# Moving the expert selection, the up bias and one weight split in a fixed engine order, and gathering the first expert in two steps

## The chip, the cores and the metric

One core of a Trainium2 chip runs the whole kernel. TensorE multiplies (its weight loads are listed apart), VectorE (DVE) and ScalarE (ACT) work elementwise, GpSimd (POOL) issues the scatter, and SyncE (SP) issues nearly all weight transfers on one in-order queue. The metric is device microseconds of one execution, the median of the runs. Before the change it is 1568.97 us (1568.40, 1568.97 and 1569.36).

## The reference

The computation is a decoder block for 512 tokens of width 1024: two mixing branches, a merge and a projection, then a mixture of experts with 32 experts of which each token takes four. Only the second half matters here:

```
h2 = rms_norm(x) * (1 + sc2) + sh2
logits = h2 @ w_router + b_router                  # 512 x 32
top 4 logits per token, softmax over them = gates
for each expert e, on the tokens that chose it:
    hu = h2 @ w_up[e] + b_up[e]                    # 1024 -> 2048, even columns x_glu, odd x_lin
    act = clamp(x_glu) * sigmoid(1.702 * x_glu) * (clamp(x_lin) + 1)
    y = act @ w_down[e] + b_down[e]                # 1024 -> 1024
    x[token] += g2 * gate * y
```

Weights and inputs are float32, and each expert has 8 MB of up weights and 4 MB of down weights.

## The kernel before

**Number format.** A float32 product is made of three float16 products: each operand is split into a high and a low half. A weight slab of 1 MB arrives in a staging slot (`st`). `split` (lines 330 to 345) lets ACT write the high half into another slot (line 341), then VectorE the low half (line 342); then the staging slot is free. Each expert has eight up slabs and four down slabs. The last down slab is multiplied in float32 without a split, so there are eleven splits per expert.

**Slots.** There are 18 slots of 8 KB per partition: the names `slot`, `slotb` and `slotc`. At most twelve hold staged weights; the others hold the split halves. A transfer is issued as soon as its slot is free (`pump`), in the order of use, so SP's queue waits for whatever frees that slot.

**Routing.** 512 tokens are four tiles of 128. For each tile `logits` projects, transposes and multiplies with the router, `choose` takes the four largest, builds a one-hot matrix and counts each token's place `pos` within its expert, `make_h2` writes the normalised tokens in two halves (the low half on GpSimd, line 997), and `gates` makes the softmax.

**Gather.** `select(e)` builds a one-hot matrix `sel` (tokens x 96 places) on VectorE (line 1125). `pick` multiplies h2 with it, 64 matmuls in four banks (line 1106), which ACT copies to `xg` (line 1113). Four small matmuls and three VectorE operations give the token index and gate.

**Expert loop.** For expert e, eight steps `up_k` accumulate in four banks `pu` that ACT has filled with the bias (`up_bias`, line 1138). At steps k = 2, 4, 5, 6 and 7 one piece of the next expert's gather is put in: the selection first, then its four banks. `swiglu` (lines 1153 to 1167) turns `pu` into `act`. Then `down_j` runs for the expert before (lines 1184 and 1192), with one `up_bias` after each of its four slabs, and `finish` writes y (line 1204), which GpSimd adds to the output by an indirect transfer (line 1196). At each step `ahead` splits the next slab, about six steps before its use.

**Order.** Up to `open_banks` a planner orders the instructions. From the mark behind `open_banks` on, every instruction of TensorE, VectorE and ACT is chained to the one written before it for the same engine. What is written first runs first.

Of the kernel before, what the change touches and what calls it, by code (L numbers as in the profile page):

```python
# [10 lines left out]
F32 = mybir.dt.float32  # L11
F16 = mybir.dt.float16
BF = mybir.dt.bfloat16
I32 = mybir.dt.int32
# [9 lines left out]
NT = 4  # L24
# [17 lines left out]
def block_body(tc, x, c, positions, w_ada, b_ada, norm1_gain, w_in, lower_bound_logits, hg_norm_gain,  # L42
# [19 lines left out]
    with top:  # L62
# [21 lines left out]
        def free(t):  # L84
            free_slots.append(t)
            staged[0] -= 1
            pump()
# [244 lines left out]

        def split(key, n, view_in=None, view_hi=None, keep=False):

            st = ready.pop(key)
            slot, hl = hl_take()
            src = st[:, :n] if view_in is None else view_in(st)
            hi, lo = hl[:, :n], hl[:, 2048:2048 + n]
            if view_hi is not None:
                hi, lo = view_hi(hi), view_hi(lo)  # L340
            A.activation(hi, src, AF.Copy, scale=SW)  # L341
            V.scalar_tensor_tensor(lo, src, SW, hi, op0=OP.mult, op1=OP.subtract)  # L342
            free(st)
            hlmap[key] = hl
            hlslot[key] = slot

        def hl_done(key):
# [570 lines left out]
        iota_c = moe.tile([128, 128], F32, name="iota_c")  # L918
        G.iota(iota_c, pattern=[[1, 128]], base=0, channel_multiplier=0, allow_small_or_imprecise_dtypes=True)
        tokn = wk.tile([128, NT], F32, name="tokn")  # L920
# [57 lines left out]

        def choose(t):
# [7 lines left out]
            pb = sd_bank()  # L987
# [3 lines left out]
            V.tensor_scalar(pos[:, t, :], pos[:, t, :], -1.0, None, op0=OP.add)  # L991
# [45 lines left out]

        def split_up(e, k):
            split(("up", e, k), 2048, view_in=lambda t: t.rearrange("p (f g) -> p g f", g=2),
                  view_hi=lambda t: t.rearrange("p (g f) -> p g f", g=2))  # L1040
# [8 lines left out]

        def ahead(i):  # L1050
            while cut[0] < len(order) and cut[0] <= i + LOOK and free_slots:
                o = order[cut[0]]
                if o[0] == "up":
                    split_up(o[1], o[2])
                elif o[2] < 3:
                    split(o, 2048)
                cut[0] += 1
# [6 lines left out]
        bias_dn()  # L1064
        pre(0)
        for t in range(NT):
            logits(t, ((0, D),) if t < NT - 1 else LAST)
# [7 lines left out]
        choose(NT - 1)  # L1075
        make_h2(NT - 1)
        if "lg" in dbg:
            G.dma_start(dbg["lg"], lg)
            G.dma_start(dbg["h2"], h2)

        if "pos" in dbg:
            G.dma_start(dbg["pos"], pos)
            G.dma_start(dbg["aux"], aux)
        w2p.close()
        psA.close()
        moe = top.enter_context(tc.tile_pool(name="moeb", bufs=1, reuse_waits="tile"))


        more_slots(moe, "slotc", NSC, NS + NSB + NSC - NHX)
        pse = top.enter_context(tc.tile_pool(name="pse", bufs=1, space=PSUM, reuse_waits="tile"))  # L1090
        pu = [pse.tile([128, 512], F32, name=f"pu{i}") for i in range(4)]
        pd = [pse.tile([128, 512], F32, name=f"pd{i}") for i in range(2)]

        def pick(sel, auxv):
# [5 lines left out]
            for part in range(2):  # L1100
                for u in range(2):
# [12 lines left out]
                    if not (part and u):  # L1114
                        yield None
            a = bk[:C, 4 * C:4 * C + 3]
# [4 lines left out]
            yield xg, gate[:, 2:3], idx  # L1121

# [6 lines left out]
        def open_banks():  # L1129

            z = moe.tile([128, 512], F16, name="sg_g", bufs=2)
            V.memset(z, 0.0)
            for i in range(4):
                T.matmul(pu[i], lhsT=z[:, :128], rhs=z, start=True, stop=True)

# [11 lines left out]

        def swiglu(act, act32):
            n = 4 * C
            g, l, s = [], [], []  # L1150
            for hf in range(2):
                g.append(moe.tile([128, n], F32, name="sg_g", bufs=2))
                V.tensor_scalar(g[hf], pu[hf][:, :n], 1.702 / SU, 7.0 * 1.702, op0=OP.mult, op1=OP.min)
                s.append(moe.tile([128, n], F32, name="sg_s", bufs=2))
                A.activation(s[hf], g[hf], AF.Silu)
            for hf in range(2):
                l.append(act32.rearrange("p k c -> p (k c)") if hf else moe.tile([128, n], F32, name="sg_l"))
                V.tensor_scalar(l[hf], pu[2 + hf][:, :n], -7.0 * SU, 7.0 * SU, op0=OP.max, op1=OP.min)
            parts = []
            for hf in range(2):  # L1160
# [48 lines left out]
        def overflow_table():  # L1209
# [9 lines left out]
            while C * q < S:  # L1219
# [10 lines left out]
            V.tensor_tensor(cmpt, iota_c[:, :NB, None].to_broadcast([128, NB, NE]),  # L1230
                            cum[:, None, :].to_broadcast([128, NB, NE]), op=OP.is_ge)
            eix = moe.tile([128, NB], F32, name="eix")
# [11 lines left out]
            V.tensor_sub(beg, iota_c[:, :NB], beg)  # L1244
            V.tensor_scalar(beg, beg, 1.0, float(C), op0=OP.add, op1=OP.mult)
            hl_give(slot)
# [16 lines left out]
        traced = nc.cur_bb.bb.instructions  # L1263
        marks = {}
        mark = traced[-1]
        first = prepare(0)
        next(first)
        gates(NT - 1)
        for _ in first:
            pass  # L1270
        for b in range(4):
            up_bias(bu[:, 0], b)
        i = 0
        for e in range(NEX + 1):
            if e < NEX:
                xg, gate, idx = state[e]
                prep = prepare(e + 1) if e + 1 < NEX else iter(())
# [7 lines left out]
            if e < NEX:  # L1285
# [4 lines left out]
            if e == 0:  # L1290
                for b in range(4):
                    up_bias(bu[:, 1], b)
            if e == NEX:
                tables = overflow_table()
            if e > 0:
                _, gate, idx = state.pop(e - 1)
                down_bias(E64[:, e - 1:e])
                for j in range(4):
                    ahead(i)
                    key = ("dn", e - 1, j)  # L1300
                    if j >= 3:
                        down_j(ready[key], j, *acts[e - 1])
                        free(ready.pop(key))
                    else:
# [6 lines left out]
                acts.pop(e - 1)  # L1311


        begin = next(n for n in reversed(range(len(traced))) if traced[n] is mark) + 1
# [11 lines left out]
        with tc.For_i(0, nreg, 1) as it:  # L1326
# [4 lines left out]
            ohb = moe.tile([128, NE], F32, name="ovo")  # L1331
            V.tensor_scalar(ohb, iota_c[:, :NE], col[:, 0:1], None, op0=OP.is_equal)
            pm = moe.tile([128, NT, NE], F32, name="ovm")
# [86 lines left out]
```

## Time and profile before

| what | value |
|---|---|
| median of the runs | 1568.97 us |
| profiled execution, its own time | 1569.14 us |
| its span, first to last instruction | 1567.3 us |
| mean granted TensorE clock | 0.984 of full speed |
| busy: TensorE, weight loads, VectorE, ACT, GpSimd | 90%, 66%, 84%, 67%, 21% |
| bytes read from HBM | 463.22 MB |
| start of the first expert's first up matmul | 452.44 us |

The routing of the last tile ends at about 446 us, the expert loop takes the time from there to 1553 us, and the rest is the last scatter. In the steady part of the loop one expert follows the other every 34 us. A row of a timeline gives the start, the duration, the engine, the line, the operation, output<-inputs, shapes and a count; in brackets stands how long the engine was idle before it and what it waited for.

### The profile page before, as it was taken

To read this page: it belongs to the slowest core of one execution; us is meant where nothing else is said; L and a number is where in the kernel's file an instruction comes from. 1 tells how busy PE (TensorE), PEld (TensorE's weight loads), DVE (VectorE), ACT (ScalarE), POOL (GpSimd) and SP (SyncE) were. 2 spreads that over 40 slices of the span, in tenths; PEclk is the share of its full clock that TensorE was granted. 3 is DMA by queue.
4 is the path that set the end of the run, shared out by engine and by line. 5 is a ranking of instruction groups with operands and counts; after the bars stand their busy time and mean duration, and the time that the engine had idled before them with its cause. 6 is when DMAs were issued, how large, how long until landed. Compare 5 with 4: busy or idle time off the path is not lost. (4 is left out here: it accounts for less than half of the span.)

```text
span 1567.3 us, 41129 instructions
## 1 busy us (share of the span) xinstructions
PE 1406.7 (90%) x18200; PEld 1036.1 (66%) x18200; DVE 1310.0 (84%) x1458; ACT 1052.6 (67%) x1022; POOL 331.5 (21%) x83
## 2 busy tenths in 40 slices
PE   4989999999948999999999999999989999999996
PEld 2546566445448777777777777777777777777783
DVE  6875675877977889998898999898989889898985
ACT  4555326423457778787778787877878787887871
POOL 1010000011110022233222233322223322222310
PEclk9999999999978999999999999999999999999998
DMA  9813312669368999999999999999999999999970
GB/s 319 274 54 97 105 42 72 214 216 321 148 245 307 342 387 367 383 383 378 380 382 373 378 384 382 377 377 376 377 382 378 381 378 389 378 373 372 384 287 15
DMA packets 113520, 476.44 MB, mean 304 GB/s; under 512 B 10717, under 2 KB 35386, under 8 KB 80538
## 3 DMA queue, kind: packets, MB, share of 16 engines
q1 hardware_dynamic: 106160, 458.78, 75.7%
q0 software_dynamic: 5440, 12.72, 3.8%
q8 instruction: 144, 2.36, 0.6%
q10 hardware_dynamic: 1738, 2.27, 0.4%
q14 instruction: 38, 0.31, 0.1%
HBM read 463.22 MB, written 14.70 MB: 305 GB/s over the span
## 5 line engine op out<-in xcount | busy, mean ns | idle before, releaser
L1196 POOL DMA_INDIRECT out_dram<-y,idx x32 | 296.0, 9249 | 814.0 <-DVE y L1204 779.3
L1145 PE MATMUL pu<-xg,slot 128*128 128x96 f16 x6192 | 283.2, 207 | 25.5 <-ACT pu L1138 25.1
L342 DVE SCALAR_TENSOR_TENSOR slot<-slot,slot 128x2048 f16<-128x2048 f32 (+1 forms) x111 | 252.0, 2272 | 55.3 <-ACT slot L341 51.4
L1145 PEld LDWEIGHTS <-slot 128*128 128x128 f16 x6192 | 272.0, 98 | 36.4 <-issue 33.8
L341 ACT ACTIVATE slot<-slot 128x2048 f16<-128x2048 f32 (+1 forms) x111 | 224.3, 2022 | 51.8 <-DVE slot L342 22.9
L1192 PEld LDWEIGHTS <-act 128*96 128x96 f16 x1152 | 139.1, 123 | 114.2 <-issue 13.2
L1145 PE MATMUL pu<-xg,slotc 128*128 128x96 f16 x4032 | 185.8, 207 | 12.3 <-ACT pu L1138 12.2
L1145 PEld LDWEIGHTS <-slotc 128*128 128x128 f16 x4032 | 177.9, 98 | 19.5 <-issue 19.5
L1106 PE MATMUL gb<-sel,h 128*128 128x96 f16 x2048 | 109.2, 207 | 49.3 <-DVE sel L1125 48.8
L695 PE MATMUL mm<-hT,slot 128*128 128x512 f16 x672 | 151.5, 380 | 0.0
L342 DVE SCALAR_TENSOR_TENSOR slotc<-slot,slotc 128x2048 f16<-128x2048 f32 x56 | 128.3, 2292 | 27.0 <-ACT slotc L341 24.5
L342 DVE SCALAR_TENSOR_TENSOR slot<-slotb,slot 128x2048 f16<-128x2048 f32 x61 | 138.6, 2286 | 13.2 <-ACT slot L341 12.0
L341 ACT ACTIVATE slot<-slotb 128x2048 f16<-128x2048 f32 x61 | 118.9, 1953 | 26.8 <-PE pu L1145 23.8
L1106 PEld LDWEIGHTS <-h 128*128 128x128 f16 x2048 | 94.4, 98 | 54.5 <-DVE sel L1125 53.3
L1192 PE MATMUL pd<-slot,act 128*96 128x512 f16 x552 | 123.9, 380 | 0.0
L341 ACT ACTIVATE slotc<-slot 128x2048 f16<-128x2048 f32 x56 | 116.2, 2075 | 8.5 <-PE pu L1145 8.5
L695 PEld LDWEIGHTS <-slot 128*128 128x128 f16 x672 | 65.7, 98 | 77.7 <-issue 3.1
L342 DVE SCALAR_TENSOR_TENSOR slotc<-slotb,slotc 128x2048 f16<-128x2048 f32 x42 | 95.5, 2286 | 12.7 <-ACT slotc L341 12.3
L1145 PE MATMUL pu<-xg,slotb 128*128 128x96 f16 x2064 | 95.7, 206 | 6.2 <-ACT pu L1138 6.1
L1145 PEld LDWEIGHTS <-slotb 128*128 128x128 f16 x2064 | 90.7, 98 | 9.8 <-issue 9.8
L1184 PE MATMUL pd<-slot,act 128*96 128x512 f32 x216 | 97.1, 592 | 0.0
L341 ACT ACTIVATE slotc<-slotb 128x2048 f16<-128x2048 f32 x42 | 81.8, 1953 | 17.4 <-PE pu L1145 16.1
(328 smaller groups left out, 2058.4 us busy)
## 6 DMA issues: line engine op xcount, KB each, us to landing
slot<-in_w_up_dram SPq DMA_DIRECT2D x164, 1024.0 KB, 6.9
slotb<-in_w_down_dram SPq DMA_DIRECT2D x98, 1024.0 KB, 10.9
slotc<-in_w_up_dram SPq DMA_DIRECT2D x62, 1024.0 KB
slotb<-in_w_up_dram SPq DMA_DIRECT2D x30, 1024.0 KB, 9.3
slot<-in_w_down_dram SPq DMA_DIRECT2D x30, 1024.0 KB, 5.6
slot<-in_w_in_dram SPq DMA_DIRECT2D x16, 1024.0 KB, 5.2
slot<-in_w_ada_dram SPq DMA_DIRECT2D x16, 1024.0 KB, 5.3
slot<-in_w_ada_dram SPq DMA_DIRECT2D x16, 512.0 KB, 9.9
```

The lines of the kernel that those rows point to most:

```text
L341: A.activation(hi, src, AF.Copy, scale=SW)
L342: V.scalar_tensor_tensor(lo, src, SW, hi, op0=OP.mult, op1=OP.subtract)
L695: T.matmul(bk, lhsT=hl[:, o:o + 128], rhs=hT[:, ph, k, :], start=(k == 0 and n == 0), stop=(k == KT - 1 and n == 2))
L1106: T.matmul(bk[:, C * k:C * k + C], lhsT=h2[:, part, t, 128 * kk:128 * kk + 128], rhs=sel[:, t, :], start=(k == 0 and t == 0), stop=(t == N ...
L1145: T.matmul(o, lhsT=hl[:, 2048 * pw + 128 * f:2048 * pw + 128 * f + 128], rhs=xg[:, pa_, k, :], start=False, stop=(k == KT - 1 and n == 2), ...
L1184: T.matmul(pd[u][:C, :], lhsT=act32[:, k - 4, :], rhs=w[:, o:o + 512], start=False, stop=(k == KT - 1))
L1192: T.matmul(pd[u][:C, :], lhsT=act[:, pa_, k, :], rhs=w[:, c0:c0 + 512], start=False, stop=False)
L1196: G.indirect_dma_start(out=out2, out_offset=bass.IndirectOffsetOnAxis(ap=idx[:n, :1], axis=0), in_=y[:n, :], in_offset=None, bounds_check= ...
```

## The change

- **The place is counted from one.** `iota_c` starts at 1 and `choose` keeps `pos` without taking one off; the overflow code is adapted. One VectorE operation per tile goes, and so does a memset in `open_banks`.
- **The fixed order begins earlier**, ahead of the first gather and of the last tile's choice.
- **The first gather is done in two steps.** The selection of expert 0 for tiles 0 to 2 (`select0`, in a slot of its own) and 48 of the 64 gather matmuls stand before the choice of the last tile, the other 16 after it, in the two `gb` and the two `pd` banks. The last tile's h2 is made in halves, its low half on VectorE. Two slabs are split around this: the high halves ahead of it, the low halves behind the four evictions. The small matmuls for index and gate come at step k = 4 of expert 0, followed by one dummy Silu.
- **The second gather** (expert 1) is put between the clamps and the Silus of expert 0's `swiglu`, with its bias.
- **Every later expert:** the selection of expert e + 2 stands behind `swiglu` of expert e; the gather's four banks are at k = 2, 4, 5 and 6. The split that stood at the first down slab has its high half ahead of `swiglu` and its low half behind it. The four biases stand at the first two down slabs, two at each, ahead of the multiplication.

```diff
-        def split(key, n, view_in=None, view_hi=None, keep=False):
+        def split(key, n, view_in=None, view_hi=None, later=None):
...
-            V.scalar_tensor_tensor(lo, src, SW, hi, op0=OP.mult, op1=OP.subtract)
-            free(st)
...
+            def low():
+                V.scalar_tensor_tensor(lo, src, SW, hi, op0=OP.mult, op1=OP.subtract)
+                free(st)
+            if later is None:
+                low()
+            else:
+                later.append(low)
...
+        def make_h2_halves(t):
+            xa, rs = xas.pop(t), rss.pop(t)
+            halves = [slice(0, 512), slice(512, 1024)]
+            for sl in halves:
+                V.scalar_tensor_tensor(xa[:, sl], xa[:, sl], rs[:, 1:2], s2row[:, sl], op0=OP.mult, op1=OP.add)
+                A.activation(h2[:, 0, t, sl], xa[:, sl], AF.Copy)
+            yield
+            for sl in halves:
+                V.tensor_sub(h2[:, 1, t, sl], xa[:, sl], h2[:, 0, t, sl])
...
+        sel0slot, sel0 = hl_take()
...
+        lows = []
+        ahead(cut[0] - LOOK, lows)
+        ahead(cut[0] - LOOK, lows)
+        gather0(0, NT - 1)
+        halves = make_h2_halves(NT - 1)
+        choose(NT - 1, pu[3], lambda: next(halves))
+        select0(NT - 1, NT)
+        for _ in halves:
+            pass
...
         open_banks()
+        gather0(NT - 1, NT)
         for b in range(4):
             up_bias(bu[:, 0], b)
+            A.activation(xg[...], gbs[2 * q + u][:, :4 * C], AF.Copy)
+        for low in lows:
+            low()
+        gates(NT - 1)
+        nexts = {1: prepare(1)}
+        next(nexts[1])
...
-                    if k in PICK_AT:
+                    if e > 0 and k in PICK_AT:
                         next(prep, None)
                     up_k(hlmap[("up", e, k)], k, xg)
...
+                lows = []
+                ahead(i, lows)
+                acts[e] = new_act()
+                swiglu(*acts[e], read=rest if e == 0 else None)
+                for low in lows:
+                    low()
                 for _ in prep:
                     pass
-                acts[e] = new_act()
-                swiglu(*acts[e])
+                if e + 2 < NEX:
+                    nexts[e + 2] = prepare(e + 2)
+                    next(nexts[e + 2])
...
                 for j in range(4):
                     ahead(i)
+                    if j < 2 and e < NEX - 1:
+                        up_bias(bu[:, e + 1], 2 * j)
+                        up_bias(bu[:, e + 1], 2 * j + 1)
...
-                    if e < NEX - 1:
-                        up_bias(bu[:, e + 1], j)
```

## Rows read from the trace of the kernel before

**Rows 1.** Window of the steady loop: length, busy PE, PEld, DVE, ACT, POOL, clock, DMA share, GB/s.

```profile
534.00:1520.00 986.00, 912.14 (x14443) 731.17 (x14444) 883.49 (x725) 778.51 (x667) 289.71 (x29) 1.00 0.97 379
```

**Rows 2.** Waits, 520 to 1500 us: waiter <- releaser: total us, times, longest.

```profile
PE gb L1106 <- DVE sel L1125: 39.1, 29, 1.4
PE pu L1145 <- ACT pu L1138: 35.0, 29, 1.3
```

**Rows 3.** Waits of SP's queue, the same stretch.

```profile
SPq L158 <- DVE slot L342: 259.1, 87, 7.4
```

**Rows 4.** Timeline of one expert in the steady loop.

```profile
986.99 2.29 DVE L342 SCALAR_TENSOR_TENSOR slot<-slot,slot 128x2048 f16<-128x2048 f32 x1 [0.43 <-ACT slot L341]
...
989.52 1.01 DVE L1153 TENSOR_SCALAR sg_g<-pu 128x384 f32<-128x384 f32 x2
990.10 0.99 ACT L1155 ACTIVATE sg_s<-sg_g 128x384 f32<-128x384 f32 x2 [2.77 <-DVE sg_g L1153]
...
992.69 2.05 ACT L341 ACTIVATE slot<-slot 128x2048 f16<-128x2048 f32 x1
...
994.65 0.47 ACT L1138 ACTIVATE pu<-bu 128x384 f32<-128x384 f32 x1
994.77 4.67 DVE L342 SCALAR_TENSOR_TENSOR slot<-slot,slot 128x2048 f16<-128x2048 f32 x2 [1.43 <-ACT slot L341]
...
999.41 1.69 PE L1145 MATMUL pu<-xg,slotb 128*128 128x96 f16 x36
...
1002.32 0.67 PE L1145 MATMUL pu<-xg,slotb 128*128 128x96 f16 x12 [1.22 <-ACT pu L1138]
...
1007.13 3.94 ACT L341 ACTIVATE slot<-slotb 128x2048 f16<-128x2048 f32 x2
...
1009.85 0.55 DVE L1125 TENSOR_TENSOR sel<-iota_c,pos 128x384 f16<-128x384 f32 x1
...
1010.46 0.85 PE L1106 MATMUL gb<-sel,h 128*128 128x96 f16 x16 [1.33 <-DVE sel L1125]
```

**Rows 5.** Windows around that period, columns as in rows 1.

```profile
995.00:1001.00 6.00, 6.00 (x50) 3.38 (x49) 5.82 (x3) 6.00 (x6) 0.00 (x0) 1.00 0.67 257
1001.00:1029.00 28.00, 25.45 (x453) 21.83 (x450) 24.74 (x24) 20.95 (x19) 10.30 (x1) 1.00 1.01 397
```

**Rows 6.** SP's timeline of that period: start, time from first to last issue.

```profile
978.63 5.39 SPq L162 DMA_DIRECT2D slotb<-in_w_down_dram  x3
...
989.30 15.26 SPq L158 DMA_DIRECT2D slot<-in_w_up_dram  x5
```

**Rows 7.** The page's DMA issues: KB each, median us to landing.

```profile
slotb<-in_w_down_dram SPq DMA_DIRECT2D x98, 1024.0 KB, 10.9
```

**Rows 8.** Timeline from the last tile's choice to the second expert.

```profile
444.69 1.20 DVE L991 TENSOR_SCALAR pos<-pos 128x32 f32<-128x32 f32 x1
...
447.89 3.45 PE L1106 MATMUL gb<-sel,h 128*128 128x96 f16 x64
...
452.44 6.28 PE L1145 MATMUL pu<-xg,slot 128*128 128x96 f16 x144 [0.96 <-ACT pu L1138]
...
455.64 4.49 DVE L342 SCALAR_TENSOR_TENSOR slotc<-slotb,slotc 128x2048 f16<-128x2048 f32 x2 [3.19 <-ACT slotc L341]
457.96 11.37 SPq L162 DMA_DIRECT2D slotb<-in_w_down_dram  x4
...
469.46 1.46 PE L1106 MATMUL gb<-sel,h 128*128 128x96 f16 x16 [8.70 <-DVE sel L1125]
...
484.10 1.01 DVE L1153 TENSOR_SCALAR sg_g<-pu 128x384 f32<-128x384 f32 x2
...
513.09 1.01 DVE L1153 TENSOR_SCALAR sg_g<-pu 128x384 f32<-128x384 f32 x2
```

**Rows 9.** Timeline near the end.

```profile
1500.55 1.01 DVE L1153 TENSOR_SCALAR sg_g<-pu 128x384 f32<-128x384 f32 x2
...
1532.85 1.01 DVE L1153 TENSOR_SCALAR sg_g<-pu 128x384 f32<-128x384 f32 x2
```

More of the change, by code (lines that the diff above doesn't have):

```diff
@@ L977, in logits, with choose @@
             G.dma_start(out2[128 * t:128 * t + 128, :], x1)
-        def choose(t):
+        def choose(t, bank=None, between=None):
             V.max(tv[:, t, :], lg[:, t, :])
@@ L986, in choose @@
                 V.tensor_reduce(Mb[:, t, :], oh[:, t].rearrange("p k e -> p e k"), axis=AX.X, op=OP.add)
-            pb = sd_bank()
+            if between is not None:
+                between()
+            pb = sd_bank() if bank is None else bank
             for u in range(t + 1):
@@ L1036, in bias_dn, with split_up @@
             free(st)
-        def split_up(e, k):
-            split(("up", e, k), 2048, view_in=lambda t: t.rearrange("p (f g) -> p g f", g=2),
+        def split_up(e, k, later=None):
+            split(("up", e, k), 2048, later=later, view_in=lambda t: t.rearrange("p (f g) -> p g f", g=2),
                   view_hi=lambda t: t.rearrange("p (g f) -> p g f", g=2))
@@ L1048, in block_body, with ahead @@
         cut = [0]
-        def ahead(i):
+        def ahead(i, later=None):
             while cut[0] < len(order) and cut[0] <= i + LOOK and free_slots:
@@ L1053, in ahead @@
                 if o[0] == "up":
-                    split_up(o[1], o[2])
+                    split_up(o[1], o[2], later)
                 elif o[2] < 3:
-                    split(o, 2048)
+                    split(o, 2048, later=later)
                 cut[0] += 1
@@ L1065, in block_body, with select0 @@
         pre(0)
+        sel0slot, sel0 = hl_take()
+        sel0 = sel0[:, :NT * C].rearrange("p (t c) -> p t c", t=NT)
+        def select0(t0, t1):
+            V.tensor_tensor(sel0[:, t0:t1], iota_c[:, None, :C].to_broadcast([128, t1 - t0, C]),
+                            pos[:, t0:t1, 0:1].to_broadcast([128, t1 - t0, C]), op=OP.is_equal)
         for t in range(NT):
+            if t == NT - 1:
+                select0(0, NT - 1)
             logits(t, ((0, D),) if t < NT - 1 else LAST)
@@ L1074, in block_body @@
             hl_done(("wo", j))
[L1075 to L1084, printed above, removed]
         psA.close()
-        moe = top.enter_context(tc.tile_pool(name="moeb", bufs=1, reuse_waits="tile"))
-        more_slots(moe, "slotc", NSC, NS + NSB + NSC - NHX)
         pse = top.enter_context(tc.tile_pool(name="pse", bufs=1, space=PSUM, reuse_waits="tile"))
@@ L1092, in block_body, with gather0 @@
         pd = [pse.tile([128, 512], F32, name=f"pd{i}") for i in range(2)]
+        gbs = [pse.tile([128, 512], F32, name="gb", bufs=2) for _ in range(2)] + pd
+        traced = nc.cur_bb.bb.instructions
+        mark = traced[-1]
+        def gather0(t0, t1):
+            for q, bk in enumerate(gbs):
+                part, u = divmod(q, 2)
+                for t in range(t0, t1):
+                    for k in range(4):
+                        kk = 4 * u + k
+                        T.matmul(bk[:, C * k:C * k + C], lhsT=h2[:, part, t, 128 * kk:128 * kk + 128],
+                                 rhs=sel0[:, t, :], start=(k == 0 and t == 0), stop=(t == NT - 1),
+                                 skip_group_check=True)
+        lows = []
[7 more added lines that the diff above has]
+            pass
+        w2p.close()
+        moe = top.enter_context(tc.tile_pool(name="moeb", bufs=1, reuse_waits="tile"))
+        more_slots(moe, "slotc", NSC, NS + NSB + NSC - NHX)
         def pick(sel, auxv):
@@ L1115, in pick, with slots_of @@
                         yield None
-            a = bk[:C, 4 * C:4 * C + 3]
+            slots_of(bk[:C, 4 * C:4 * C + 3], gate, idx)
+            yield xg, gate[:, 2:3], idx
+        def slots_of(a, gate, idx):
             V.tensor_scalar(idx[:C], a[:, 0:1], 1024.0, None, op0=OP.add)
@@ L1129, in open_banks @@
         def open_banks():
-            z = moe.tile([128, 512], F16, name="sg_g", bufs=2)
-            V.memset(z, 0.0)
             for i in range(4):
-                T.matmul(pu[i], lhsT=z[:, :128], rhs=z, start=True, stop=True)
+                T.matmul(pu[i], lhsT=h2[:, 0, 0, :128], rhs=h2[:, 0, 0, :512], start=True, stop=True)
         def up_bias(b, i):
@@ L1146, in up_k, with swiglu @@
                              start=False, stop=(k == KT - 1 and n == 2), skip_group_check=True)
-        def swiglu(act, act32):
+        def swiglu(act, act32, read=None):
             n = 4 * C
@@ L1158, in swiglu @@
                 V.tensor_scalar(l[hf], pu[2 + hf][:, :n], -7.0 * SU, 7.0 * SU, op0=OP.max, op1=OP.min)
+            if read is not None:
+                read()
+            for hf in range(2):
+                s.append(moe.tile([128, n], F32, name="sg_s", bufs=2))
+                A.activation(s[hf], g[hf], AF.Silu)
             parts = []
@@ L1262, in block_body, with rest @@
         open_banks()
[L1263 to L1270, printed above, removed]
+        xg = moe.tile([128, 2, KT, C], F16, name="xg", bufs=2)
+        gate = moe.tile([128, 4], F32, name="gate", bufs=4)
+        idx = moe.tile([128, 1], I32, name="idx", bufs=4)
+        gather0(NT - 1, NT)
         for b in range(4):
             up_bias(bu[:, 0], b)
+            q, u = (0, 1, 0, 1)[b], (0, 0, 1, 1)[b]
+            A.activation(xg[:, q, 4 * u:4 * u + 4, :].rearrange("p k c -> p (k c)"), gbs[2 * q + u][:, :4 * C],
+                         AF.Copy)
+        for low in lows:
+            low()
+        gates(NT - 1)
+        state[0] = xg, gate[:, 2:3], idx
+        nexts = {1: prepare(1)}
+        next(nexts[1])
+        def rest():
+            for b in range(4):
+                if b % 2 == 0:
+                    for _ in range(3):
+                        next(prep, None)
+                up_bias(bu[:, 1], b)
         i = 0
@@ L1284, in block_body @@
                     i += 1
-            if e < NEX:
+                    if e == 0 and k == 4:
+                        for t in range(NT):
+                            T.matmul(gbs[3][:C, 4 * C:4 * C + 3], lhsT=sel0[:, t, :], rhs=aux[:, t, 0, :], start=False,
+                                     stop=(t == NT - 1), skip_group_check=True)
+                        slots_of(gbs[3][:C, 4 * C:4 * C + 3], gate, idx)
+                        hl_give(sel0slot)
+                        A.activation(gate[:, 3:4], bu[:, 0, 0:1], AF.Silu)
+                lows = []
[4 more added lines that the diff above has]
+                    low()
                 for _ in prep:
                     pass
-                acts[e] = new_act()
-                swiglu(*acts[e])
-            if e == 0:
-                for b in range(4):
-                    up_bias(bu[:, 1], b)
+                if e + 2 < NEX:
+                    nexts[e + 2] = prepare(e + 2)
+                    next(nexts[e + 2])
             if e == NEX:
@@ L1311, in block_body @@
                 acts.pop(e - 1)
+        marks = {}
         begin = next(n for n in reversed(range(len(traced))) if traced[n] is mark) + 1
```

16 lines of the change are left out of this document (6 added, 10 removed).

## The prediction

> **What bounds the kernel now.** I read the windows first. Over 986 us of the expert loop, 29 periods of 34.0, the DMA engines are 97% busy at 379 GB/s; per period TensorE is busy 912.14 / 29 = 31.45 us, VectorE 30.47 and ACT 26.85 [rows 1]. The reader is to see four resources close together and none full. The period is the distance between two `sg_g`: (1500.55 - 513.09) / 29 = 34.05 us [rows 8, 9].
>
> The waits come next, to see who is late. TensorE has two: for the selection (39.1 us in 29 times, 1.35 per expert) and for the last bias (35.0 in 29, 1.21) [rows 2]. Their sum, 2.56, is the whole difference of 34.0 to TensorE's 31.45. No engine waits for a weight transfer; SP's queue waits for VectorE to free a slot [rows 3].
>
> The timeline shows the chain behind both. VectorE finishes the low half of step 7 (986.99 + 2.29), starts `sg_g` at 989.52, the Silus follow, only then ACT writes the next high half (992.69), and VectorE stands idle 1.43 us before the low half at 994.77. It runs without a pause to the selection, and TensorE gets its first gather matmul at 1010.46, 1.33 late. The biases stand behind four high halves on ACT, so TensorE waits 1.22 us at 1002.32 [rows 4].
>
> The transfers have little room. Between `sg_g` and the next free slot SP issues nothing, and the DMA share falls to 0.67 for 6 us; in the 28 us after it is 1.01 at 397 GB/s [rows 5]. A full stream would therefore need 34.05 x 379 / 397 = 32.5 us per expert. But there is a lead: the down slabs issued from 978.63 on [rows 6] land 10.9 us later [rows 7], at 989.5, and ACT first reads them at 1007.13 [rows 4], 17.6 us later. (Twelve staged slabs put ten splits and the float32 slab between issue and use, so these are the same slabs.)
>
> **The steady loop, part by part.**
>
> Selection behind the swiglu before: the same 0.55 us on VectorE, no longer between low halves that TensorE's gather waits for. The 1.35 goes. Its place behind the deferred low half is covered by a whole up phase. The four gather banks come one step earlier; TensorE does the same 64 matmuls, and ACT copies each bank behind a high half as now.
>
> Bias at the first two down slabs: four times the same ACT operation, now ahead of three of the four high halves. `pu` was read by the clamps by then. The last bias ends at about 992.69 + 4 x 0.47 + 2.05 = 996.6, ahead of the first up matmul at 999.41 [rows 4]. The 1.21 goes. It costs the next high halves up to 1.9 us on ACT; VectorE, 1.43 ahead by the next item, hides it but for some 0.5.
>
> High half before `swiglu`, low half after: ACT now waits 2.77 us for `sg_g` [rows 4]; a high half takes 2.05. This is an added wait: the Silus, the act copies and the biases queue behind it on ACT, and the slot it writes is that of step 7, so it starts when `pu` is complete. VectorE first finishes the low half of step 7, which hides it; if VectorE were early, the Silus would be up to 2.05 - 0.55 = 1.5 late. VectorE's idle 1.43 goes. Bounds: -1.43 to +1.5; I take -1.43 + 0.5.
>
> What is late next: TensorE's pure work is 31.45, VectorE's 30.47 + 0.5 = 31.0. A slab is split about six steps ahead of its use; a step with its gather bank is about 1.69 + 0.67 + 0.85 = 3.2 us, one without 2.4, so six are some 17, and the split takes 2.05 + 2.3. Small differences between the two engines are absorbed. The engines alone would give 31.5. The stream's 32.5 then decides, but only after the lead: it shrinks by 1.0 per expert and lasts about 17 experts. 17 at 31.5 and 12 at 32.5 give 31.9; I take 32.1 for slots that come free unevenly. Bounds: 31.45 (TensorE) and 34.05 (nothing won).
>
> A rule of the Trainium skill speaks against this: "DMA: Bandwidth & Descriptors", section Specifications, gives a core about 358 GB/s of HBM as its limit. By it the stream at 379 could not get faster and the loop would stay at 34.05. The trace does not agree: it shows 397 over 28 us [rows 5].
>
> **The transition.** One VectorE operation per tile goes, 1.20 us at the last [rows 8], with a memset. The low half of the last h2 moves from GpSimd to two VectorE operations in halves. Ahead of the last choice stand 48 matmuls; 64 take 3.45 [rows 8], so 2.6 at full clock and 5.2 at half. TensorE stands idle while VectorE chooses, which hides them, but the choice's four counting matmuls queue behind them: between 0 and 5.2 us of delay if their banks come free late. I take 2. Two high halves (4.1 us of ACT) fit its gaps before the last choice; at worst they delay an eviction by one, 2 us. The fourth bank-opening matmul waits for `pos`, with the last 16 gather matmuls behind it; 16 take 0.9. The first up matmul, at 452.44 now, comes some 3 us earlier: 1.4 from VectorE, 2.6 from the gather, 1 from interleaving four copies and four biases (two of 0.47), less the 2.
>
> More is won on VectorE. The low halves of the fourth and fifth slab run at 455.64 now; behind the choice they run from about 447, 8 us earlier, and with them the first free slot and SP's next transfer (457.96 [rows 8]). TensorE's wait of 8.70 us for the second selection at 469.46 is gone, and VectorE, which works through eleven low halves up to `sg_g` at 484.10, becomes the bound of expert 0. The second gather adds four copies and four biases (8 x 0.47 = 3.8 us) ahead of the Silus on ACT, with the swiglu behind them, and about 2.5 us of idle VectorE. But TensorE then starts expert 1 earlier than now by about what was won before. Expert 0's slot costs one prefetched slab (1 MB, 2.7 us), which lands in the idle of the queue. `slotc` is opened behind the choice, so SP's last two prefetches may come some 3 us later; they are used 20 us on. I put `sg_g` of expert 1 (513.09) at 501: -12. Bounds: 0 (the 8 us lost again to 5.2, 2 and the copies) and -17 (8 + 8.7).
>
> The tail is bound by TensorE as before: from `sg_g` of the last expert (1532.85 [rows 9]) to the end 34.4 us; one operation less, nothing.
>
> **Sum.** Profiled time 1569.14 (span 1567.3, 1.84 outside). Less 12, less 29 x 1.95 = 56.6, less 1.0 for the last period, 32.3 now: 1499.5. The median lies 0.17 below the profiled time: 1499.
>
> **Rivals.**
>
> *The stream binds at once.* The lead is used up early by the uneven restart, and the period is 32.5 to 33.1 (share 1.00 in place of 0.97). For it: 0.95 to 1.01 is near full already. Against: 17.6 us of lead. With 32.8: 1569 - 12 - 36 - 1 = 1520.
>
> *Only the transition.* The loop stays near 34.05 because another wait of the fixed order takes over, TensorE for a low half, say, or because the stream gives no more than 379. For it: four resources within 10%. Against: the two waits sum to all of TensorE's idle time, and 397 is there. 1569 - 12 = 1557. The limit in the Trainium skill's "DMA: Bandwidth & Descriptors", Specifications, would end here.
>
> *Slower.* The high half ahead of the Silus reads a slab. Once the lead is gone, ACT may stand there until the slab lands, the Silus and all of VectorE behind it; no slot comes free for 2.05 + 3.8 + 2.3 = 8.2 us (high half; swiglu, 989.52 to 994.77 - 1.43; low half). If fewer than three transfers of 32.5 / 12 = 2.7 are then queued, two say, the stream idles 2.8 us in each period: 32.5 + 2.8 = 35.3. It decides when the lead is zero and the queue is below three. For it: today's stream runs dry in just that place [rows 5]. Against: a late stream means that free slots are many and the queue is long. 1569 - 12 + 29 x 1.25 = 1593.
>
> **How the numbers follow.** Forecast 1499, own range 1484 to 1512: 0.50. Stream at once, 1512 to 1535: 0.25. Only the transition, 1540 to 1562: 0.10. Better than 1484 (31.5 throughout and 17 at the start: 1476): 0.07. Slower: 0.06. No change, 1566 to 1572: 0.02. The range runs from 1478 to 1553, and leaves out most of the last three and half of the third, under 0.2. A measurement of this kernel tells about 0.2% from no change, 3 us: faster 0.92, same 0.02, slower 0.06.
>
> **What would show it.** Right: no wait of TensorE for `sel` or for `pu` from ACT in the loop; a `sg_g` period of 31.5 first and 32.5 late; DMA share 1.0 and above 390 GB/s; ACT waiting for transfers only late; `sg_g` of expert 1 near 501; the first free slot near 449. Wrong: a period above 33.5, new waits of TensorE for low halves, or ACT waiting for slabs from the first experts on.

## The result and the profile after

The changed kernel takes 1501.73 us (median of four runs, 1500.85 to 1504.53); the kernel before took 1568.83 beside it (1568.40 to 1569.36). The ratio is 0.9575, with a 95% interval of 0.9559 to 0.9592: 67.1 us less, where 70 were forecast. The profiled execution took 1501.85 us, with a span of 1500.1 and a granted clock of 0.986 of full speed.

The distances between the `sg_g` divide the gain, with rows of before from [rows 8, 9]:

| part | before | after | difference | forecast |
|---|---|---|---|---|
| start of the span to `sg_g` of expert 1 | 513.09 | 500.55 | -12.5 | -12 |
| 29 periods | 987.46 | 928.82 | -58.6 | -56.6 |
| last period | 32.30 | 34.99 | +2.7 | -1.0 |
| last `sg_g` to the end of the span | 34.4 | 35.7 | +1.3 | 0 |

The windows of the steady loop come first, with the columns of [rows 1].

```profile
500.00:1440.00 940.00, 923.00 (x14603) 741.22 (x14601) 885.87 (x737) 791.61 (x679) 320.83 (x29) 1.00 1.01 399
500.00:970.00 470.00, 465.11 (x7417) 375.02 (x7416) 449.69 (x372) 401.96 (x344) 160.99 (x15) 1.00 1.01 402
970.00:1440.00 470.00, 457.89 (x7191) 366.19 (x7188) 436.18 (x366) 389.65 (x335) 159.84 (x14) 1.00 1.01 396
```

TensorE now works 923 of 940 us, on average 923.00 x 32.03 / 940 = 31.45 us per expert, as before. That is not its least: the period from 500.55 to 531.62, without a pause of TensorE, is 31.07 us long. The DMA engines have gone from a share of 0.97 at 379 GB/s to 1.01 at 399. In the first half TensorE is idle for 4.9 us, in the second for 12.1.

Next, the waits from 500 to 1440 us of TensorE, then of ACT (as in [rows 2]: total, times, longest).

```profile
PE pu L1190 <- issue: 9.3, 19, 0.9
PE pu L1190 <- DVE sel L1172: 2.9, 3, 1.6
...
PE pu L1190 <- ACT pu L1183: 1.0, 2, 0.7
```

```profile
ACT sg_s L1207 <- DVE sg_g L1199: 13.4, 22, 0.8
ACT slot L341 <- DMA slot<-in_w_up_dram: 13.1, 11, 2.7
ACT slot L341 <- DMA slotc<-in_w_up_dram: 9.9, 7, 3.1
```

The selection's 39.1 us and the bias's 35.0 [rows 2] are 2.9 and 1.0. For the 9.3 us of the first row the profile shows no cause. New are ACT's waits for weights. None falls between 500 and 900 us. Between 900 and 1000 there is this one:

```profile
ACT slotb L341 <- DMA slot<-in_w_up_dram: 0.9, 1, 0.9
```

SP's queue waited for VectorE to free a slot [rows 3]. Now it waits for earlier transfers as well, and the page's landing time of a down slab has doubled from 10.9 us [rows 7]:

```profile
SPq L158 <- DVE slot L346: 234.8, 105, 5.6
SPq L158 <- DMA slotb<-in_w_down_dram: 106.6, 51, 3.3
```

```profile
slotb<-in_w_down_dram SPq DMA_DIRECT2D x98, 1024.0 KB, 21.6
```

One expert in the timeline shows the new order, to be held beside [rows 4].

```profile
500.55 1.01 DVE L1199 TENSOR_SCALAR sg_g<-pu 128x384 f32<-128x384 f32 x2
...
501.13 0.99 ACT L1207 ACTIVATE sg_s<-sg_g 128x384 f32<-128x384 f32 x2 [0.82 <-DVE sg_g L1199]
...
504.29 2.29 DVE L346 SCALAR_TENSOR_TENSOR slotb<-slot,slotb 128x2048 f16<-128x2048 f32 x1
...
506.49 0.55 DVE L1172 TENSOR_TENSOR sel<-iota_c,pos 128x384 f16<-128x384 f32 x1
...
513.97 0.84 PE L1150 MATMUL gb<-sel,h 128*128 128x96 f16 x16
...
531.62 1.01 DVE L1199 TENSOR_SCALAR sg_g<-pu 128x384 f32<-128x384 f32 x2
```

The low half at 504.29 has no bracket: VectorE's idle 1.43 us at that place is gone, ACT's 2.77 ahead of the Silu has shrunk to 0.82, and the selection is ready 7 us before its gather. The next `sg_g` follows after 31.07 us.

The transition, beside [rows 8]; its first row holds the last router matmuls:

```profile
440.20 0.29 PE L976 MATMUL sd<-wrs,xat 128*128 128x32 f16 x4 [0.22 <-DVE xat L972]
...
446.39 2.29 DVE L346 SCALAR_TENSOR_TENSOR slot<-slotb,slot 128x2048 f16<-128x2048 f32 x1
...
446.71 0.25 PE L1190 MATMUL pu<-xg,slot 128*128 128x96 f16 x2
...
447.16 8.24 PE L1190 MATMUL pu<-xg,slot 128*128 128x96 f16 x190 [0.21 <-ACT xg L1320]
...
453.43 6.98 SPq L162 DMA_DIRECT2D slotb<-in_w_down_dram  x4
...
473.16 2.72 PE L1150 MATMUL gb<-sel,h 128*128 128x96 f16 x32 [8.00 <-ACT xg L1157]
...
473.60 1.02 DVE L1199 TENSOR_SCALAR sg_g<-pu 128x384 f32<-128x384 f32 x2
```

The end, beside [rows 9]:

```profile
1457.71 1.91 ACT L341 ACTIVATE slotb<-slot 128x2048 f16<-128x2048 f32 x1 [4.93 <-DMA slot<-in_w_down_dram]
...
1459.65 2.29 DVE L346 SCALAR_TENSOR_TENSOR slotb<-slot,slotb 128x2048 f16<-128x2048 f32 x1 [3.61 <-ACT slotb L341]
...
1464.36 1.02 DVE L1199 TENSOR_SCALAR sg_g<-pu 128x384 f32<-128x384 f32 x2
...
1471.10 1.24 PE L1225 MATMUL pd<-bd,E 64*96 64x512 f16 x2 [7.37 <-DVE y L1253]
...
1472.27 7.83 PE L1241 MATMUL pd<-slotb,act 128*96 128x512 f16 x24
```

ACT stands 4.93 us for a down slab of the last expert, VectorE 3.61 behind it, and the last `swiglu`, which needs none of these slabs, is written behind them. TensorE then stands idle for 7.37 us, and its 24 matmuls take 7.83 us where the same number took 5.38 in the loop: the granted clock from 1471 to 1480 is 0.65.

### The profile page after: what moved, and what is told of

It reads as the page before. It is cut to its first block, busy times and chain, and to the rows that moved or that the text cites. A ratio compares the mean times of both kernels' runs of the same rounds, so it can differ in the third digit from the quotient of the medians.

```text
span 1500.1 us, 41126 instructions
## 1 busy us (share of the span) xinstructions
PE 1402.3 (93%) x18200; PEld 1035.1 (69%) x18200; DVE 1299.1 (87%) x1457; ACT 1053.5 (70%) x1024; POOL 358.4 (24%) x82
## 5 line engine op out<-in xcount | busy, mean ns | idle before, releaser
L1190 PE MATMUL pu<-xg,slot 128*128 128x96 f16 x10224 | 463.2, 206 | 10.5 <-issue 7.0
L1190 PEld LDWEIGHTS <-slot 128*128 128x128 f16 x10224 | 446.0, 98 | 28.6 <-issue 23.7
L346 DVE SCALAR_TENSOR_TENSOR slot<-slotb,slot 128x2048 f16<-128x2048 f32 x101 | 227.7, 2282 | 8.2 <-ACT slot L341 7.9
L346 DVE SCALAR_TENSOR_TENSOR slot<-slotc,slot 128x2048 f16<-128x2048 f32 x97 | 219.7, 2283 | 12.6 <-ACT slot L341 12.4
L341 ACT ACTIVATE slot<-slotc 128x2048 f16<-128x2048 f32 x97 | 201.5, 2104 | 31.4 <-DMA slotc<-in_w_up_dram 9.9
L341 ACT ACTIVATE slot<-slotb 128x2048 f16<-128x2048 f32 x101 | 197.4, 1957 | 32.0 <-PE pu L1190 11.4
L1241 PE MATMUL pd<-slot,act 128*96 128x512 f16 x924 | 206.4, 380 | 0.0
L701 PEld LDWEIGHTS <-slot 128*128 128x128 f16 x672 | 65.5, 98 | 77.8 <-issue 2.9
L1150 PE MATMUL gb<-sel,h 128*128 128x96 f16 x1984 | 106.3, 208 | 11.7 <-ACT xg L1157 8.0
L1157 ACT ACTIVATE xg<-gb 128x384 f16<-128x384 f32 x124 | 59.1, 477 | 1.6 <-PE gb L1150 1.4
L1183 ACT ACTIVATE pu<-bu 128x384 f32<-128x384 f32 x128 | 57.0, 477 | 0.0
L346 DVE SCALAR_TENSOR_TENSOR slotb<-slot,slotb 128x2048 f16<-128x2048 f32 x20 | 45.8, 2289 | 11.6 <-ACT slotb L341 11.5
## 6 DMA issues: line engine op xcount, KB each, us to landing
slotb<-in_w_down_dram SPq DMA_DIRECT2D x98, 1024.0 KB, 21.6
```

The source lines that it names most:

```text
L701: T.matmul(bk, lhsT=hl[:, o:o + 128], rhs=hT[:, ph, k, :], start=(k == 0 and n == 0), stop=(k == KT - 1 and n == 2))
L1150: T.matmul(bk[:, C * k:C * k + C], lhsT=h2[:, part, t, 128 * kk:128 * kk + 128], rhs=sel[:, t, :], start=(k == 0 and t == 0), stop=(t == N ...
L1157: A.activation(xg[:, part, 4 * u:4 * u + 4, :].rearrange("p k c -> p (k c)"), bk[:, :4 * C], AF.Copy)
L1183: A.activation(pu[i][:, :4 * C].rearrange("p (m c) -> p m c", m=4), b[:, 4 * i:4 * i + 4, None].to_broadcast([128, 4, C]), AF.Copy)
L1190: T.matmul(o, lhsT=hl[:, 2048 * pw + 128 * f:2048 * pw + 128 * f + 128], rhs=xg[:, pa_, k, :], start=False, stop=(k == KT - 1 and n == 2), ...
L1241: T.matmul(pd[u][:C, :], lhsT=act[:, pa_, k, :], rhs=w[:, c0:c0 + 512], start=False, stop=False)
```

## The experiments

Diffs are against the changed kernel unless the text says otherwise. The three edits of the loop are called the selection edit (the selection behind the swiglu before), the bias edit (at the first two down slabs) and the split edit (high half ahead of `swiglu`, low half behind). The kernel before took 1568.50 us beside the first four runs, 1568.38 beside the next four and 1567.73 beside the last four.

### All three loop edits undone, the new start kept

```diff
-prep = nexts.pop(e + 1, iter(()))
+prep = nexts.pop(e + 1) if e == 0 else prepare(e + 1) if e + 1 < NEX else iter(())
...
-ahead(i, lows)                       # ahead of swiglu
+if e == 0:
+    ahead(i, lows)
...
-if e + 2 < NEX:
-    nexts[e + 2] = prepare(e + 2)
-    next(nexts[e + 2])
...
-if j < 2 and e < NEX - 1:
-    up_bias(bu[:, e + 1], 2 * j)
-    up_bias(bu[:, e + 1], 2 * j + 1)
...
+if e < NEX - 1:                       # behind each down_j
+    up_bias(bu[:, e + 1], j)
```

> The three edits of the steady loop are undone (selection at k = 2, one bias after each down slab, the split at the first down slab whole behind the swiglu); the start keeps its change. Theory (the gain per expert comes from these three): the sg_g period is 34.0 again, both waits of TensorE are back, and only the start's 12 us are left: 1569 - 12 = 1557 us, 1550 to 1562. Rival (the loop runs faster because it enters with more slabs split or staged): the period stays at 32 to 33 without the three edits, 1502 to 1530 us.

Measured: 1556.84 us, ratio 0.9925 (0.9908 to 0.9942). The period is 34.02, and the waits from 540 to 1400 us are back:

```profile
PE gb L1150 <- DVE sel L1172: 32.3, 25, 1.4
PE pu L1190 <- ACT pu L1183: 28.8, 25, 1.3
```

The start alone is worth 11.7 us and nothing is given back later. This is also the time that the rival "only the transition" named; the changed kernel is 55 us faster.

### The loop edits alone, on the kernel before

The kernel before with the three loop edits, its start left as it was.

> The kernel before with the three edits of the steady loop alone; routing, first gather, second gather and the places counted from zero stay as before. Theory (the start's 12 us and the loop's gain add up; the loop's gain comes from the edits): sg_g of expert 1 stays near 513, the period is 31.5 first and about 32.5 late: 1502 + 12 = 1514 us, 1509 to 1519. Rival (the loop needs the early start: with VectorE and the queue as far behind as before at expert 1, the lead is used up at once): 32.5 to 33 throughout, 1525 to 1540 us.

Measured: 1511.75 us, ratio 0.9639 (0.9622 to 0.9656). `sg_g` of expert 1 is at 512.22, the mean period 32.01. The loop is worth 56.6 us without the new start and 55.1 behind it: start and loop add up, within 1.5 us.

### Each loop edit undone by itself

The same hunks as above, one at a time: the selection's, the bias's, the split's.

> Only the selection goes back to k = 2 with its gather banks at k = 4 to 7; bias and split stay changed. Theory (the wait for the selection is on the loop's path): TensorE waits about 1.35 us per expert again, the engines' period is 31.5 + 1.35 = 32.85, above the stream's 32.5, so the whole loop goes at 32.85: 1502 + 29 x 0.8 = 1526 us, 1518 to 1532. Rival (VectorE comes to the selection earlier now, so that the wait was gone by the other two edits alone): the period stays at 32.0, 1500 to 1506 us.

> Only the biases go back to one after each of the four down slabs. Theory (the bias wait is on the path): TensorE waits 1.2 us at the last bias again, the engines' period is 32.7, just above the stream: 1502 + 29 x 0.65 = 1521 us, 1514 to 1528. Rival (ACT is ahead now because one high half was taken out from between the biases, so the last bias comes 2 us earlier and in time): no wait, 1500 to 1505 us.

> Only the split at the first down slab goes back behind the swiglu as a whole, for every expert but the first. Theory (VectorE and TensorE nearly bind together): VectorE is idle 1.4 us per expert again, its period is 30.5 + 1.4 + 0.5 = 32.4, about the stream's; the first 15 experts lose 0.9 each, the later ones nothing: 1502 + 14 = 1516 us, 1508 to 1520. Rival A (VectorE has slack): 1500 to 1505. Rival B (it is a wait in series for all experts): 29 x 1.4 = 41, 1543 us.

Measured: 1515.37 us without the selection edit (0.9669, 0.9653 to 0.9685), 1500.02 without the bias edit (0.9558, 0.9542 to 0.9574), 1511.12 without the split edit (0.9638, 0.9622 to 0.9654). The first wait is of the kernel without the selection edit, the second without the bias edit, the third and fourth without the split edit.

```profile
PE gb L1150 <- DVE sel L1172: 36.8, 26, 1.5
```

```profile
PE pu L1190 <- ACT pu L1183: 2.2, 2, 1.2
```

```profile
ACT sg_s L1207 <- DVE sg_g L1199: 131.3, 26, 5.3
...
PE pu L1190 <- ACT pu L1183: 15.6, 21, 1.1
```

So 13.6 us come back with the selection's wait and 9.4 with the split, but nothing with the biases: back in their old place they are in time. For the biases the rival came true and for the split the theory. For the selection the time lies between the two: the period of 32.69 costs 29 x 0.66 = 19.1 us, but the last period is 30.99 instead of 34.99 and the tail 1.9 us shorter. The three losses sum to 21 us, and undoing all three costs 55. The edits do not add up, so each was also tried alone.

### Each loop edit alone, the new start kept

> Changed start; of the three edits of the loop only the split ahead of and behind the swiglu is kept (selection and biases as before). From the runs so far: without the selection edit the period is 32.69 with a wait of 1.41 for the selection; without the bias edit nothing is lost. Theory (a high half less between the biases brings the last bias in time, so the bias edit is worth nothing wherever the split edit stands): period 32.7, 1515 us, 1512 to 1520. Rival (the edits add up, 1.2 more for the bias): period 33.9, 1550 us.

> Changed start; of the three edits only the biases at the first two down slabs are kept. Theory (the loop's path runs from TensorE's step 6 over VectorE's chain to the selection and back; the bias wait lies beside it): TensorE waits for the selection 2.5 us in place of 1.35, the period stays at 34.0, 1556 us, 1552 to 1562. Rival (the waits are in series): 34.0 - 1.2 = 32.8, 1520 us.

> Changed start; of the three edits only the early selection is kept. Theory (the selection is the edge of the path; with it gone TensorE waits only for the last bias, 1.2): period 31.45 + 1.2 = 32.65, 1520 us, 1512 to 1526. Rival (VectorE's chain binds anyway through the low halves): period 33.5 to 34, 1545 to 1557 us.

Measured: the split edit alone 1510.66 us (0.9637, 0.9621 to 0.9653), 1.3 below the range of its theory, the bias edit alone 1637.09 (1.0440, 1.0423 to 1.0458), the selection edit alone 1540.53 (0.9830, 0.9813 to 0.9846). All eight combinations, behind the new start:

| split edit | neither | selection | bias | both |
|---|---|---|---|---|
| without | 1556.84 | 1540.53 | 1637.09 | 1511.12 |
| with | 1510.66 | 1500.02 | 1515.37 | 1501.73 |

The split edit alone brings 46 of the 55 us. In its trace the selection's wait is left (first fence), the bias's has no row, and ACT waits for no transfer. The stream keeps up at a share of 1.01 and 397 GB/s from 540 to 1400 us (second fence), with a landing of 12.5 us for a down slab (third).

```profile
PE gb L1150 <- DVE sel L1172: 31.0, 27, 1.2
```

```profile
540.00:1400.00 860.00, 828.01 (x13181) 665.60 (x13180) 805.26 (x660) 718.35 (x609) 57.37 (x27) 1.00 1.01 397
```

```profile
slotb<-in_w_down_dram SPq DMA_DIRECT2D x98, 1024.0 KB, 12.5
```

The period is 32.48, about TensorE's 31.27 (828.01 x 32.48 / 860) and a wait of 1.15. The bias wait goes with the split edit, in whose order ACT has one high half less between `swiglu` and the biases. Beside the split edit alone, the bias edit costs 4.7 us (1510.66 to 1515.37).

The bias edit alone makes the kernel slower than before, and both its theory (1556) and its rival (1520) missed that. Waits from 540 to 1400 us, the timeline of one place, and the clock behind it:

```profile
DVE slot L346 <- ACT slot L341: 113.9, 107, 2.9
...
PE gb L1150 <- DVE sel L1172: 77.3, 23, 3.4
```

```profile
1000.39 0.55 DVE L1172 TENSOR_TENSOR sel<-iota_c,pos 128x384 f16<-128x384 f32 x1
...
1000.99 1.46 PE L1150 MATMUL gb<-sel,h 128*128 128x96 f16 x16 [3.38 <-DVE sel L1172]
...
1002.25 4.04 PE L1190 MATMUL pu<-xg,slot 128*128 128x96 f16 x48
...
1007.04 2.20 PE L1190 MATMUL pu<-xg,slot 128*128 128x96 f16 x48
```

```profile
998.00:1001.00 3.00, 0.01 (x1) 0.01 (x1) 3.00 (x4) 1.81 (x2) 3.00 (x1) 0.80 0.98 396
1001.00:1006.00 5.00, 5.00 (x63) 5.00 (x64) 4.34 (x2) 0.49 (x1) 5.00 (x1) 0.50 1.01 428
```

With the biases ahead of the high halves and the split still in its old place, VectorE waits 113.9 us for high halves (64.4 with all three edits undone), the selection comes 3.38 us late instead of 1.33 [rows 4], and behind that pause the granted clock is 0.50, the lower level of 1.2 GHz: 48 matmuls take 4.04 us instead of 2.20. With the selection edit beside it there is no such pause, and the same bias edit gains 29 us (1540.53 to 1511.12). Of the selection edit alone, between its theory and its rival, the trace shows that the bias wait grew to 36.0 us in 26 times.

### A quarter less of most up slabs

From expert 4 on, only 1536 of the 2048 columns of each up slab are transferred. The rest of the slot keeps older numbers, so this part of the weights is left out. The engines do the same work.

```diff
+n = 2048 if e < 4 else 1536
 queue(("up", e, k), lambda t: SP.dma_start(
-    t, dview(w_up, (e * 1024 + 128 * k) * 2048, [[2048, 128], [1, 2048]])))
+    t[:, :n], dview(w_up, (e * 1024 + 128 * k) * 2048, [[2048, 128], [1, n]])))
```

> The changed kernel, but each up slab from expert 4 on is transferred only in its first 1536 of 2048 columns (10 MB per expert in place of 12; the rest of the slot keeps older numbers, all compute is the same). Theory (late in the loop the stream binds; early the engines do): the early period stays at 31.5, the late one falls from 32.5 to 31.5, ACT waits for no slab, and the last period is no longer 35.0 but about 31.5: 1502 - 14 - 3.5 = 1484 us, 1479 to 1488. Rival (the late periods have another cause, or the transfers slow all engines): unchanged 1500 to 1504, or early periods below 31.2 and under 1475.

Measured: 1483.99 us (1479.1 to 1489.8), ratio 0.9454 (0.9427 to 0.9481). ACT waits for no transfer. The window late in the loop:

```profile
960.00:1400.00 440.00, 435.26 (x6971) 351.71 (x6970) 421.44 (x350) 376.27 (x322) 131.81 (x14) 1.00 0.95 343
```

The last 14 periods have a mean of 31.52 instead of 32.49, and the last one is 31.0 instead of 35.0. The late 32.5 and the long last period are thus the stream's. The shortest of the 29 periods is 31.09, in the changed kernel 31.07, so less stream does not make the engines faster. The first 15 periods have a mean of 31.93, more than the 31.60 of the changed kernel; the profiled execution took 1489.80 us. About half of the periods are 31.1, and four are 32.7 to 35.5; in one of them TensorE's row reads

```profile
694.71 0.67 PE L1191 MATMUL pu<-xg,slotb 128*128 128x96 f16 x12 [2.52 <-issue]
```

and from 696 to 700 us the granted clock is 0.52 to 0.63. What TensorE waited for there the profile does not show; these periods stay open.

### At most nine staged slabs instead of twelve

```diff
-NHX = 6
+NHX = 9
```

> The changed kernel with at most 9 staged slabs in place of 12 (three more slots for split halves, of which the six-step lookahead uses at most one or two). Theory (the lead of issue before use carries the first half of the loop; three slabs less are 3 x 2.7 = 8 us of it): the period of 31.5 lasts for about half as many experts, then 32.5: 1502 + 8 = 1510 us, 1505 to 1514. Rival A (what is late in the loop does not come from a used-up lead): 1500 to 1503. Rival B (with nine slabs the queue runs dry in each period): over 1520 us.

Measured: 1510.18 us, ratio 0.9630 (0.9609 to 0.9650). The total is the expected one, but not its place. `sg_g` of expert 1 comes at 510.63, 10.1 us late; the 29 periods have a mean of 32.13 instead of 32.03, 3.0 us in sum. What did move is where ACT begins to wait for transfers. Between 900 and 1000 us, where the changed kernel had 0.9 us in one wait, it has 11.7 in twelve, the largest group being

```profile
ACT slot L341 <- DMA slot<-in_w_up_dram: 7.2, 4, 3.3
```

The lead can be read from the trace: in the changed kernel a down slab of expert 2 (counted from 0) lands 15.6 us before ACT reads it, and this time falls to 0.1 us at expert 21. Here it is 9.1 us at expert 2 and 0.2 at expert 12. The first 12 periods have a mean of 31.56, the other 17 one of 32.53. So a smaller stock ends earlier, as the theory of the lead says. Its price cannot be read from this run, since the start alone lost more than the 8.5 us between the two kernels.

### The first gather in one step

Without `gather0(0, NT - 1)` ahead of the last choice; all 64 matmuls stand behind it.

> The changed kernel with all 64 matmuls of the first gather behind the last choice, none ahead of it. Theory (VectorE bounds expert 0, so the gather's 2.6 us are not on its path): the first up matmul comes about 2.6 us later, sg_g of experts 0 and 1 at the same time as now: 1500 to 1503 us. Rival (the first up matmul sets the start): 1502 + 2.6 = 1504.5, 1503.5 to 1506 us.

Measured: 1502.26 us, ratio 0.9587 (0.9563 to 0.9612), not to be told from the changed kernel. TensorE's rows, from the last router matmuls to the first up matmul:

```profile
438.05 0.29 PE L976 MATMUL sd<-wrs,xat 128*128 128x32 f16 x4 [0.22 <-DVE xat L972]
...
445.12 1.52 PE L1120 MATMUL pd<-slot,h 128*128 128x96 f16 x32
...
446.48 2.71 PE L1189 MATMUL pu<-xg,slot 128*128 128x96 f16 x60
```

The routing ahead of this place has the same code, but ended 2.15 us earlier in this execution (438.05 for 440.20). Counted from there, the first up matmul comes after 8.4 us, in the changed kernel after 6.5, and after 6.5 to 6.7 in all ten other runs with the two steps. So the two steps bring it forward by 1.9 us, of the 2.6 that the prediction gave them. `sg_g` of expert 0 comes 34.7 us after the last router matmuls instead of 33.4; whether any of this reaches the total, the spread of the runs (1500.07 to 1506.38) does not tell.

### The last swiglu ahead of its own down slabs

For the last expert, splits of its own down slabs no longer stand ahead of `swiglu`: two come behind it, the third ahead of the overflow table.

```diff
-def ahead(i, later=None):
-    while cut[0] < len(order) and cut[0] <= i + LOOK and free_slots:
+def ahead(i, later=None, end=999):
+    while cut[0] < end and cut[0] < len(order) and cut[0] <= i + LOOK and free_slots:
...
+last = order.index(("dn", NEX - 1, 0))
...
-ahead(i)                              # in the up steps
+ahead(i, None, last if e == NEX - 1 else 999)
...
-ahead(i, lows)
+ahead(i, lows, last if e == NEX - 1 else 999)
...
-ahead(i)                              # in the down steps
+ahead(i, None, last + 2 if e == NEX - 1 else 999)
...
+ahead(i)
 tables = overflow_table()
```

> The changed kernel with another order at the last expert: its swiglu no longer stands behind the splits of its own three down slabs, whose transfers land last; two of them stand behind the swiglu and the third ahead of the overflow table. Theory (the last period of 35.0 us and TensorE's wait of 7.4 us for y come from VectorE's fixed order behind late slabs): sg_g of the last expert 10 us earlier, the wait for y gone but for 2 us: 1502 - 7 = 1495 us, 1491 to 1498. Rival (the end waits for the last slab itself, whatever the order): 1500 to 1503 us.

Measured: 1495.14 us (1494.05 to 1497.24), ratio 0.9540 (0.9523 to 0.9557): the fastest of the kernels that do the whole computation.

```profile
1455.56 1.01 DVE L1199 TENSOR_SCALAR sg_g<-pu 128x384 f32<-128x384 f32 x2
...
1460.67 4.49 DVE L346 SCALAR_TENSOR_TENSOR slotb<-slot,slotb 128x2048 f16<-128x2048 f32 x2 [1.28 <-ACT slotb L341]
...
1465.87 0.37 PE L1225 MATMUL pd<-bd,E 64*96 64x512 f16 x1 [0.87 <-DVE y L1253]
```

The last `sg_g` comes 8.8 us earlier, TensorE's wait of 7.37 us is 0.87, the clock stays at full speed there, and the 24 matmuls behind it take 5.38 us instead of 7.83. The last period and the tail were indeed lost to the fixed order around late slabs.

## Why the prediction was right, point by point

**The total.** 1499 was forecast, 1501.73 measured. The mechanism held: two waits of TensorE went, the stream filled up, and the lead was used up in the course of the loop, after some 20 of its 32 experts.

**Early 31.5, late 32.5.** The first 15 periods have a mean of 31.60 (500.55 to 974.48), the last 14 one of 32.49. The lead itself stands in the trace, as the time from the landing of each expert's second down slab to ACT's reading of it: 15.6 us at expert 2, 10.8 at 8, 4.7 at 14, 1.3 at 20 and 0.1 at 21 (landed at 1153.66, read at 1153.77). In the kernel before it is 17.5 at expert 2 and 17.7 at expert 20. So it shrank by 0.8 us per expert instead of 1.0 and lasted to expert 20; 17 experts would have ended at 501 + 17 x 31.5 = 1037. The 19 periods up to expert 20 have a mean of 31.70, the ten behind it one of 32.66. Their sum comes out close to that of 17 at 31.5 and 12 at 32.5, in part because a slower early period and a longer lead offset each other. The run with less stream shows that the late part is the stream's.

**What each edit was credited with.** This step failed, though its sum came out. The prediction took 1.35 us for the selection and 1.21 for the biases off TensorE's period, and 0.93 off VectorE's for the split, and let the stream's 32.5 cap the result. The runs show that the terms are not of that kind. The bias wait goes with the split edit already, so the bias edit is worth nothing in the finished kernel and costs 80 us alone. The split edit, priced on VectorE only, brings 46 of 55 us when it is alone. And whichever single edit is left out, the period comes to 32.4 to 32.7 or stays where it was, since below 32.5 only the lead is left to win. Nor is TensorE's 31.45 a bound, as the prediction has it: the shortest periods are 31.07 and, with less stream, 31.09.

**High half ahead of the Silus.** Bounds were -1.43 to +1.5 us and -0.93 was taken. VectorE's pause is gone and ACT's wait for `sg_g` is 13.4 us in 22 times, 0.6 each; the added wait is hidden, as argued.

**The transition.** The sum held (-12.5 for -12), its terms less well. The first up matmul is 5.7 us earlier (446.71 for 452.44) instead of 3, and 6.3 when counted from the last router matmuls, which start at 439.61 in the kernel before; 1.9 of it is owed to the two-step gather. Only one low half was put off, since the second slab found no free slot: it runs at 446.39, and SP issues its next slab at 453.43 instead of about 449. `sg_g` of expert 0 is 10.5 us earlier (473.60 for 484.10 [rows 8]), and the distance from there to the next 2.0 shorter. How much of the other 4.4 falls to the missing operation, to the halves of h2 and to the earlier fixed order was not tried.

**The last period and the tail.** These were mis-sized: -1.0 and 0 were forecast, +2.7 and +1.3 measured. The prediction carried the engines' gain over to the last period and did not ask what a stream that is late by then does to the last expert, whose down slabs are split ahead of its `swiglu`. The run with the last swiglu first puts a price of 6.6 us on it.

**The rivals.** The stream did not bind at once: ACT waits for no transfer before 900 us. "Only the transition" is refuted by the 55 us of the loop, and the stream went on to 402 GB/s over 470 us. "Slower" is refuted too. ACT does stand at slabs late in the loop, up to 3.1 us, but by then SP's queue is long (a landing of 21.6 us) and the DMA share stays at 1.01.

On the limit of 358 GB/s that the prediction quoted, the trace disagrees, with those 402 GB/s. The Trainium skill's "HBM Reference", section Specifications (TRN2), sets beside it about 425 GB/s for a core that streams alone; the trace agrees with that sentence: 402 lies above 358 and below 425.

## What to carry to other kernels

When several waits sit in one fixed order, their sum says about what all edits together can win, not what each one is worth: build the combinations, since an edit that is harmless beside another can alone be the worst of all. When the engines become faster than the stream, the first gains come out of the stock of staged slabs; follow the time from landing to first use from expert to expert, and forecast a period before and one after it is used up. Then look at the end of the program: work written behind splits of late slabs that it does not need is the first to pay.

## What the runs showed of the hardware

A pause of TensorE of 3.38 us was followed by a granted clock of 0.50 over 5 us, and in the run with the bias edit alone the mean over 540 to 960 us was 0.93; pauses of 1.2 to 1.5 us for the same wait left it at 1.00. The transfers sustained 402 GB/s over 470 us, at a share of 1.01. A fuller queue shows as a longer landing (21.6 us for 10.9) at a rate that hardly rises (399 for 379).
